# A hybrid attention and recurrence block: three engines in a written order from the output projection to the first FFN tiles, and the first FFN unit's weight sums kept in DRAM

## The chip, the cores and the metric

The kernel runs on one core of a Trainium2 chip. The metric is the device time of one execution in microseconds; the result of a kernel is the median of several executions. A profile is one more execution, taken by the hardware profiler.

## The reference

One layer of a streaming encoder, 512 tokens by 1024 features, in float32:

```python
xn = rmsnorm(h, norm_mix_g)
q, k, v, xr, gr, ga, gb = split(xn @ w_in)
ya = chunked_band_attention(q, k, v, rel_table) @ w_attn_out
yb = (rg_lru(conv(xr)) * gelu(gr)) @ w_rnn_out
h = h + (sigmoid(ga) * ya + sigmoid(gb) * yb) @ w_o
hn = rmsnorm(h, norm_ffn_g)
gate, up = split(hn @ w_ffn_in)           # 2816 columns each
h = h + (silu(gate) * up) @ w_ffn_out
out = rmsnorm(h, final_norm_g)
```

What matters here is the stretch from `@ w_o` to the first columns of `hn @ w_ffn_in`.

## The kernel before

**Precision.** Each float32 factor is split in two: ScalarE writes the rounded part (`hi`, L82), VectorE the rest (`lo`, L83). `mm3` (L74 to L78) then makes three matmuls: hi·hi on L76, hi·lo on L77, lo·hi on L78. So every weight tile that is loaded costs one pass of ScalarE and one of VectorE before TensorE may use it. Weights arrive as `raw` tiles of 128x1024; three such tiles exist, and a fourth load waits until the first is split. All of these loads are issued by SyncE (SP in the profile), one behind the other: a load that waits for its tile holds up those behind it.

**Products in blocks.** The products with `w_o`, and those of the FFN from its second column pair on, use a scheme of seven block products instead of eight (Strassen's, in Winograd's form). The matrices are cut into 2x2 blocks, named 11 to 22 here, and some products use sums of blocks: s1 to s4 of one factor, t1 to t4 of the other. For `w_o` the weights' sums t1 to t4 have been made early in the kernel and stand in DRAM (`sums_o`); b11, b21 and b22 are plain blocks of `w_o`. m is the gated merge that is multiplied with them; its own sums are s1 to s4 (`m_sum`, `m_split`). For the FFN the weights' sums are s1 to s4 (`s_fg`, `s_fu`, two tiles per unit, `s21` and `s34`), made by `weight_sums` from the raw tiles with four VectorE instructions per unit, and t1 to t4 are sums of the activations.

**The stretch in question.** The products with `w_o` are written as `h_multiply` calls, each over two units u: a11·b11, a12·b21, s1·t1, s2·t2, s4·b22, s3·t3, a22·t4. Halves of h (`ht`, four tiles of 128 tokens, h0 to h3) are read out of PSUM by `h_read` (VectorE, L888). When both halves of a token tile are there, `square_h` takes its sum of squares (ScalarE, L896, `hj`), a root follows (L334), a reciprocal (L336), and VectorE scales the tile to `xs_ffn` (L342). `turned` then transposes two feature blocks (`jp`, 0, 2, 4, 6) of two token tiles into one PSUM tile (`pt_ffn`, two of them, TensorE, L349) and evicts it in six pieces: for each of the two blocks a hi by ScalarE (L353) and a lo by VectorE (L354), and a plain float32 copy (`x32`, for the sums t1 to t4) by ScalarE for the first block (L356), by VectorE for the second (L358). The evicted parts are `hn00`, `hn10` (features 0 to 511 and 512 to 1023 of the lower half, tokens of h0 and h1) and `hn01`, `hn11` (the upper half, h2 and h3).

The first FFN columns, `fg0` and `fu0`, are plain products: `project_part` makes four tiles `po_f0` to `po_f3`, each in two halves of 24 matmuls; the lower halves run first, in two parts each, with the upper half's transposes between. The upper halves follow, and then `block_product` (from L269) makes the Strassen tiles in pairs, fg2 and fu2 first. `p` and `q` are its PSUM tiles, `keepa` and `keepb` what ScalarE copies out of `p` and `q` between products, L277.

**What sets the order.** A scheduler orders the instructions of each engine by its own estimate of when they can run. Inside `tc.manual_schedule(engines=...)` the named engines keep the order in which the code is written. In this kernel only TensorE is named; VectorE, ScalarE and SP are placed by the scheduler. In the stretch before the FFN, `barrier[0] = "fg2"` holds loads behind fg2 back.

Late in the FFN, sums of blocks of `w_ffn_out` are made in units (`late`) and written to DRAM; the loop over j advances one of these with `next(steps, None)` twice per pair of tiles.

Of the kernel before, what the change touches and what calls it, by code (L numbers as in the profile page):

```python
# [36 lines left out]
def block_kernel(ctx: ExitStack, tc: tile.TileContext, x, norm_mix_g, w_in, b_merge, rel_table,  # L37
# [118 lines left out]
    begun = {}  # L156
    spare = [None]

    def weight_sums(name, ahead=False):
# [8 lines left out]
        if name not in begun:  # L168
# [3 lines left out]
            s2, s1, s3, s4 = s21[:, 0], s21[:, 1], s34[:, 0], s34[:, 1]  # L172
# [632 lines left out]
    def wo_part(name, src):  # L805
# [38 lines left out]
    for j in range(KT):  # L844
        if j >= 4 and j % 2 == 0:
            blocks_wo(("b11", "b21")[j // 2 - 2])
# [17 lines left out]
    for name in ("t1", "t2", "b22"):  # L864
        blocks_wo(name)
# [10 lines left out]
    def h_multiply(a, b, half, cc, start, tokens=range(2), us=range(2)):  # L876
        for u in us:
            x, w = m_parts[a, u], wo[f"{b}_{u}"]
            for i in tokens:
                tok = slice(i * P, (i + 1) * P)  # L880
                for k in range(2):
                    mm3(bank_of(2 * half + i, cc)[:], x[:, k, 0, tok], x[:, k, 1, tok], w[:, 0, k], w[:, 1, k],
                        start and u == 0 and k == 0, u == 1 and k == 1, parts=True)
# [8 lines left out]
    def square_h(t, cc, last):  # L892
# [4 lines left out]
        if last:  # L897
            q = cp.tile([P, 1], F32, tag="ssq", bufs=4, name=f"hsq{t}")
            dve.tensor_reduce(q[:], q2s[t][:], mybir.AxisListType.X, ALU.add)
            hsq.append(q[:])  # L900

    def finish_h(t, cc, last):
        h_read(t // 2, cc, (t // 2, cc), (t % 2,))
        square_h(t, cc, last)

    with tc.manual_schedule(engines={mybir.EngineType.PE}):
        h_multiply("a11", "b11", 1, 0, True)
        for u in range(2):
# [387 lines left out]
```

## Time and profile before

| | |
|---|---|
| median of 3 runs | 866.77 us (866.61 to 867.26) |
| profiled execution | 866.91 us |
| its span | 865.1 us, TensorE clock 0.997 |
| instructions | 13011 |

The span reaches from the first instruction to the last; the execution's own time is 1.8 us longer. The profile's engines are PE (TensorE), PEld (its weight loads), DVE (VectorE), ACT (ScalarE), POOL (GpSimd) and SP (SyncE). A row of a timeline names start, duration, engine, line, operation, and output and inputs; what stands in brackets is the time that the engine stood idle before, and what ended it. In a group of instructions "x16 | 7.6, 478" means 16 instructions, 7.6 us of busy time together, 478 ns on average.

### The profile page before, as it was taken

Reading aid. Unit: us, or ns where it says so; the run is one execution under the profiler, and the core shown is the slowest. Engines: PE = TensorE matmul, PEld = TensorE weight load, DVE = VectorE, ACT = ScalarE, POOL = GpSimd, SP = SyncE. Lnnn points to the kernel's source line nnn. Section 1 sums busy time; section 2 is a strip of 40 time slices with the busy share of each in tenths; the row PEclk is TensorE's granted clock in tenths of the full one; section 3 lists DMA queues with packets and bytes.
Section 4 is the critical chain, followed back from the end, with each engine's and each line's share of the span. In section 5 each row is a group of like instructions: output and inputs, shape, how many; then the busy total and the mean of one; then the engine's idle time right before and its main releaser. Section 6 shows DMA issues by size and latency. Waiting matters only on the chain.

```text
span 865.1 us, 13011 instructions
## 1 busy us (share of the span) xinstructions
PE 849.9 (98%) x4896; PEld 743.7 (86%) x4896; DVE 632.7 (73%) x973; ACT 505.1 (58%) x869; POOL 97.8 (11%) x135
## 2 busy tenths in 40 slices
PE   8999999999999999999999999999999999999996
PEld 6977887888888888888888888899999999988885
DVE  5789867645666656566558978998988887389973
ACT  7577696741366656576635654564655655374544
POOL 2014202200113313223200000000000001000011
PEclk9999999999999999999999999999999999999998
DMA  8585323439842213232156623857343333295602
GB/s 272 184 304 170 97 73 101 118 94 349 276 134 73 73 48 111 73 110 75 52 167 189 200 75 96 293 169 264 103 124 120 100 98 98 82 318 169 191 20 97
DMA packets 95838, 124.68 MB, mean 144 GB/s; under 512 B 6432, under 2 KB 71568, under 8 KB 95776
## 3 DMA queue, kind: packets, MB, share of 16 engines
q1 hardware_dynamic: 92096, 116.19, 41.4%
q10 hardware_dynamic: 3680, 7.67, 3.3%
q8 instruction: 38, 0.62, 0.3%
q14 instruction: 24, 0.20, 0.1%
HBM read 109.12 MB, written 14.72 MB: 143 GB/s over the span
## 4 chain that ended last, share of the span: by engine, by line
PE 88%; DVE 4%; issue 3%; DMA 2%; ACT 2%; POOL 0%; ACTq 0%; DVEq 0%
PE po_out L76 4%; PE po_out L77 4%; PE po_out L78 4%; PE o L749 2%; PE p_fu L76 2%; PE p_fu L78 2%; PE p_fu L77 2%; PE pT L729 2%; PE p_fg L78 2%; PE p_fg L77 2%; PE p_fg L76 2%; PE po_ga L76 2%; PE po_v L76 2%; PE po_q L76 2%; PE po_ga L78 2%
## 5 line engine op out<-in xcount | busy, mean ns | idle before, releaser
L718 POOL TENSOR_SCALAR p<-p,rl 128x128 f32<-128x128 f32 (+1 forms) x64 | 39.6, 637 | 166.5 <-DVE rl L716 166.4
L715 ACT ACTIVATE p<-p,m 128x128 f32<-128x128 f32 (+1 forms) x64 | 35.8, 562 | 15.3 <-DVE m L714 15.3
L1059 POOL TENSOR_TENSOR act_lo<-act,act_hi 128x1024 fp32r<-128x1024 f32 x1 | 2.4, 2415 | 301.6 <-ACT act_hi L1058 301.6
L83 DVE TENSOR_TENSOR pp<-pT,pp 128x384 fp32r<-128x384 f32 (+1 forms) x48 | 27.8, 596 | 9.8 <-ACT pp L82 9.7
L714 DVE CUSTOM_DVE_ANT_0 p<-s,bias 128x128 f32<-128x128 f32 (+1 forms) x64 | 29.2, 482 | 3.9 <-PE s L711 3.8
L83 DVE TENSOR_TENSOR whl_t<-raw_t,whl_t 128x1024 fp32r<-128x1024 f32 x24 | 29.2, 1219 | 2.8 <-ACT whl_t L82 2.8
L83 DVE TENSOR_TENSOR whl_qk<-raw_qk,whl_qk 128x1024 fp32r<-128x1024 f32 x16 | 21.7, 1359 | 11.2 <-ACT whl_qk L82 11.2
L83 DVE TENSOR_TENSOR whl_fu_s<-s_fu,whl_fu_s 128x1024 fp32r<-128x1024 f32 x20 | 24.3, 1221 | 7.0 <-ACT whl_fu_s L82 6.9
L597 DVE TENSOR_TENSOR spillf<-spillf,spillf 128x1024 f32<-128x1024 f32 x16 | 19.5, 1220 | 12.4 <-DMA spillf<-in_w_ffn_out_dram 9.7
L76 PE MATMUL po_gr<-xnT,whl_gr 128*128 128x512 f32 (+1 forms) x80 | 28.1, 352 | 0.1
L77 PE MATMUL po_xr<-xnT,whl_xr 128*128 128x512 f32 (+1 forms) x80 | 27.8, 353 | 0.0
L77 PE MATMUL po_gr<-xnT,whl_gr 128*128 128x512 f32 (+1 forms) x80 | 27.8, 348 | 0.0
L83 DVE TENSOR_TENSOR whl_fg_s<-s_fg,whl_fg_s 128x1024 fp32r<-128x1024 f32 x20 | 24.3, 1222 | 4.5 <-ACT whl_fg_s L82 4.4
L78 PE MATMUL po_gr<-xnT,whl_gr 128*128 128x512 f32 (+1 forms) x80 | 27.5, 348 | 0.0
L78 PE MATMUL po_xr<-xnT,whl_xr 128*128 128x512 f32 (+1 forms) x80 | 27.3, 346 | 0.0
L76 PE MATMUL po_xr<-xnT,whl_xr 128*128 128x512 f32 (+1 forms) x80 | 26.7, 352 | 0.6 <-ACT xnT L353 0.6
L83 DVE TENSOR_TENSOR whl_b<-raw_b,whl_b 128x1024 fp32r<-128x1024 f32 x18 | 21.9, 1218 | 7.0 <-ACT whl_b L82 6.9
L82 ACT ACTIVATE whl_t<-raw_t 128x1024 fp32r<-128x1024 f32 x24 | 25.1, 1048 | 2.5 <-PE po_out L78 1.6
L82 ACT ACTIVATE whl_b<-raw_b 128x1024 fp32r<-128x1024 f32 x18 | 18.9, 1051 | 12.3 <-DMA raw_b<-in_w_o_dram 12.1
L76 PE MATMUL po_gb<-xnT,whl_gb 128*128 128x512 f32 x64 | 25.1, 392 | 0.5 <-DVE sp_p L452 0.3
L82 ACT ACTIVATE whl_qk<-raw_qk 128x1024 fp32r<-128x1024 f32 x16 | 16.8, 1051 | 15.0 <-PE po_yb L78 8.8
L76 PE MATMUL po_ga<-xnT,whl_ga 128*128 128x512 f32 x64 | 25.3, 395 | 0.0
(386 smaller groups left out, 3251.0 us busy)
## 6 DMA issues: line engine op xcount, KB each, us to landing
raw_fg<-in_w_ffn_in_dram SPq DMA_DIRECT2D x24, 512.0 KB, 3.6
raw_fu<-in_w_ffn_in_dram SPq DMA_DIRECT2D x22, 512.0 KB, 3.5
raw_qk<-in_w_in_dram SPq DMA_DIRECT2D x32, 256.0 KB, 3.3
spillf<-in_w_ffn_out_dram SPq DMA_DIRECT2D x16, 512.0 KB, 7.2
sums<-spillf SPq DMA_DIRECT2D x16, 512.0 KB, 5.2
raw_t<-sums SPq DMA_DIRECT2D x16, 512.0 KB, 4.5
raw_b<-in_w_ffn_out_dram SPq DMA_DIRECT2D x12, 512.0 KB, 4.4
raw_xr<-in_w_in_dram SPq DMA_DIRECT2D x8, 512.0 KB, 4.6
```

The costliest lines, as they stand in the source:

```text
L76: pe.matmul(o, sh, mh, start=start, stop=False, skip_group_check=parts)
L77: pe.matmul(o, sh, ml, start=False, stop=False, skip_group_check=parts)
L78: pe.matmul(o, sl, mh, start=False, stop=stop, skip_group_check=parts)
L82: act.activation(hi, src, AF.Copy)
L83: dve.tensor_sub(lo, src, f(hi))
L597: dve.tensor_sub(out_, a_, b_)
L714: dve.tensor_tensor_reduce(prob[qb][:], scs[qb], bias[:, S - w:S], -1.0, 3e38, ALU.add, ALU.min, nmax[:, qb:qb + 1])
L715: act.activation(prob[qb][:], prob[qb][:], AF.Exp, bias=nmax[:, qb:qb + 1], scale=-1.0, accum_out=lsum[:, qb:qb + 1])
L718: pool.tensor_scalar(prob[qb][:], prob[qb][:], rl[:, qb:qb + 1], 1.0, ALU.mult, ALU.mult)
L729: pe.transpose(pt[:, at * P:(at + 1) * P], prob[qb][:, kb * P:(kb + 1) * P], ident[:])
L749: pe.matmul(po[:, S - n:S], st, pp[i][:, part, lo:lo + n], start=kb == 0 and part == 0, stop=kb == NT - 1 and part == 1)
L1059: (pool if i == 0 else dve).tensor_sub(lo[:], o[:], f(hi[:]))
```

## The change

It has seven parts.

1. The written order covers VectorE and ScalarE too, from a11·b11 to the first activations (`written.close()`).
2. The sums s1 to s4 of fg2 and fu2 are made by `spill_in` during the products with `w_attn_out` (at j = 1 and 2): two loads of 512 KB per unit, four VectorE instructions, four writes of 256 KB to DRAM (`first_sums`). Later `sums_of_first` loads them as two tiles of 512 KB.
3. b22, t1 are loaded and split ahead of the first product, in tiles of their own that earlier stages have left (`v`, `qk`), t2 ahead too; t3 and t4 one product earlier, fu0 between s2·t2 and s4·b22, where it stood at a22·t4.
4. `square_h` and the root and scaling are written one after the other (`summed_h`, `scaled_h`). In the lower half jp 0 and 2 are transposed at the same place as before, then jp 4 and 6 in the middle of a22·t4.
5. The lower FFN halves are no longer cut in two; jp 0 and 2 of the upper half stand behind the second of the four, jp 4 and 6 behind the third. Before, they stood between the parts.
6. fu2's blocks a11 and a12 get tiles as fg2's had.
7. Steps of the late sums of `w_ffn_out` begin at j = 6, where they began at j = 2.

TensorE runs as many matmuls as before. VectorE's instructions go from 969 to 962, ScalarE's from 805 to 806.

```diff
+    def spill_in(name, pl, tag, bufs):
+
+        col = chunks[index[name]][1][0][1]
+        r = [pl.tile([P, 4, CW], F32, tag=tag, bufs=bufs, name=f"spill{name}_{n}") for n in range(2)]
+        for n in range(2):
+            sp.dma_start(out=r[n][:], in_=w_ffn_in[n * S:(n + 1) * S, col:col + CW].rearrange("(k p) e -> p k e", p=P))
+        s2, s3, s4, s1 = (r[n][:, :, i * P:(i + 1) * P] for n in range(2) for i in range(2))
+        dve.tensor_add(s1, s3, s1)
+        dve.tensor_sub(s3, s2, s3)
+        dve.tensor_sub(s2, s1, s2)
+        dve.tensor_sub(s4, s4, s2)
+        for to, of in zip(first_sums[name], ((s2, s1), (s3, s4))):
+            for i in range(2):
+                sp.dma_start(out=to[:, i], in_=of[i])
+
+    def sums_of_first(name):
+        pair = tuple(sums_room.tile([P, 2, 4, P], F32, tag=tag, bufs=1, name=f"{tag}_{name}") for tag in ("s21", "s34"))
+        for t, src in zip(pair, first_sums[name]):
+            sp.dma_start(out=t[:], in_=src[:])
+        return pair
...
     for j in range(KT):
-        if j >= 4 and j % 2 == 0:
-            blocks_wo(("b11", "b21")[j // 2 - 2])
+        if j >= 4:
+            blocks_wo(("b11", "b22", "b21", "t1")[j - 4])
+        if j in (1, 2):
+            spill_in(("fg2", "fu2")[j - 1], aw, "v", 8)
...
-    for name in ("t1", "t2", "b22"):
-        blocks_wo(name)
+    blocks_wo("t2")
...
-    with tc.manual_schedule(engines={mybir.EngineType.PE}):
-        h_multiply("a11", "b11", 1, 0, True)
...
+    written.enter_context(tc.manual_schedule(
+        engines={mybir.EngineType.PE, mybir.EngineType.DVE, mybir.EngineType.Activation}))
+    h_multiply("a11", "b11", 1, 0, True)
+    for u in range(2):
+        m_split("s2", u)
+    h_read(1, 0, (0, 0))
+    blocks_wo("t3")
+    h_multiply("a12", "b21", 0, 0, True)
+    for t in range(2):
+        finish_h(t, 0)
+    for u in range(2):
+        m_split("s4", u)
+    blocks_wo("t4")
+    h_multiply("s1", "t1", 0, 1, True)
+    h_read(0, 1, (1, 1))
+    for u in range(2):
+        m_split("s3", u)
+    weights("fg0", 0)
+    h_multiply("s2", "t2", 1, 0, False)
+    h_read(1, 0, (0, 1))
+    weights("fu0", 0)
+    for t in range(2):
+        h_multiply("s4", "b22", 0, 1, False, (t,))
...
+    finish_h(0, 1)
+    sd = [summed_h(0)]
+    finish_h(1, 1)
+    xs = [scaled_h(0, sd[0])]
+    xs.append(scaled_h(1, summed_h(1)))
+    h_multiply("s3", "t3", 1, 0, False, us=(0,))
+    h_multiply("s3", "t3", 1, 0, False, (0,), us=(1,))
+    h_read(1, 0, (1, 1), (0,))
+    for jp in (0, 2):
+        turned(xs, jp, gf, hn_at, 0, "ffn", f_at)
+    h_multiply("s3", "t3", 1, 0, False, (1,), us=(1,))
+    square_h(2, 1)
+    h_read(1, 0, (1, 1), (1,))
+    square_h(3, 1)
+    split_first("fg2")
+    h_multiply("a22", "t4", 1, 0, False, (0,), us=(0,))
+    turned(xs, 4, gf, hn_at, 0, "ffn", f_at)
+    h_multiply("a22", "t4", 1, 0, False, (0,), us=(1,))
+    finish_h(2, 0)
+    turned(xs, 6, gf, hn_at, 0, "ffn", f_at)
+    xs = [scaled_h(2, summed_h(2))]
+    h_multiply("a22", "t4", 1, 0, False, (1,))
+    finish_h(3, 0)
+    xs.append(scaled_h(3, summed_h(3)))
...
+    for n in range(4):
+        first.append(mm_tile(f"po_f{n}"))
+        part_in(n, 0)
+        if n == 1:
+            act.activation(warm[:], xs[1][:, 0:1], AF.Silu)
+        for jp in ((), (0, 2), (4, 6), ())[n]:
+            turned(xs, jp, gf, hn_at, 1, "ffn", f_at)
...
-        next(steps, None)
+        if j > 4:
+            next(steps, None)
```

**ScalarE, the lower half's evictions and what stands among them.** Rows of before, from the first eviction of the second transposed pair (jp 2) on. `hn00`, `hn10` and `x32` are evictions, `hj` squares, `whl_fu0` a weight split:

```order
L353 ACTIVATE hn00_4584<-pt_ffn0_2_4679,vc_383 128x256
L356 ACTIVATE x32_0_4588<-pt_ffn0_0_4668,vc_383 128x256
L353 ACTIVATE hn00_4584<-pt_ffn0_0_4668,vc_383 128x256
L356 ACTIVATE x32_1_4589<-pt_ffn0_2_4679,vc_383 128x256
L353 ACTIVATE hn00_4584<-pt_ffn0_2_4679,vc_383 128x256
L896 ACTIVATE hj3_1_4702,hsq2_3_4701<-h3_4386 128x512
L353 ACTIVATE hn10_4586<-pt_ffn0_4_4710,vc_383 128x256
L356 ACTIVATE x32_2_4590<-pt_ffn0_4_4710,vc_383 128x256
L353 ACTIVATE hn10_4586<-pt_ffn0_4_4710,vc_383 128x256
L353 ACTIVATE hn10_4586<-pt_ffn0_6_4727,vc_383 128x256
L896 ACTIVATE hj2_0_4739,hsq2_2_4698<-h2_4385 128x512
L82 ACTIVATE whl_fu0_0_4745<-raw_fu0_0_4743 128x1024
```

The same place in the changed kernel (its lines are other ones: L361 is the old L353, L364 the old L356, L929 the old L896, L921 the old L888):

```order
L364 ACTIVATE x32_1_4664<-pt_ffn0_2_4719,vc_383 128x256
L361 ACTIVATE hn00_4659<-pt_ffn0_2_4719,vc_383 128x256
L929 ACTIVATE hj2_1_4737,hsq2_2_4736<-h2_4437 128x512
L929 ACTIVATE hj3_1_4741,hsq2_3_4740<-h3_4438 128x512
L82 ACTIVATE whl_fg2_s2_4747<-s21_fg2_4743 128x2x512
L361 ACTIVATE hn10_4661<-pt_ffn0_4_4756,vc_383 128x256
L364 ACTIVATE x32_2_4665<-pt_ffn0_4_4756,vc_383 128x256
L361 ACTIVATE hn10_4661<-pt_ffn0_4_4756,vc_383 128x256
L929 ACTIVATE hj2_0_4774,hsq2_2_4736<-h2_4437 128x512
L361 ACTIVATE hn10_4661<-pt_ffn0_6_4776,vc_383 128x256
L364 ACTIVATE x32_3_4666<-pt_ffn0_6_4776,vc_383 128x256
L361 ACTIVATE hn10_4661<-pt_ffn0_6_4776,vc_383 128x256
```

A pair's three evictions now stand together. fg2's sums are split between h3's square and jp 4, and h2's second square stands between jp 4 and jp 6, behind which it stood before; the split of fu0 is gone from here.

**VectorE, from the splits of fg0 to the read of h1.** Before (`h` rows are reads out of PSUM, `rs` and `xs` the scaling):

```order
L83 TENSOR_TENSOR whl_fg0_0_4596<-raw_fg0_0_4594,whl_fg0_0_4596 128x1024
L888 SCALAR_TENSOR_TENSOR h0_4383<-po_h2_0_4423,h0_4383 128x512
L888 SCALAR_TENSOR_TENSOR h1_4384<-po_h3_0_4430,h1_4384 128x512
L83 TENSOR_TENSOR whl_fg0_4_4601<-raw_fg0_4_4599,whl_fg0_4_4601 128x1024
L888 SCALAR_TENSOR_TENSOR h0_4383<-po_h0_1_4503,h0_4383 128x512
L899 TENSOR_REDUCE hsq0_4619<-hsq2_0_4482 128x1
L336 RECIPROCAL rs_ffn0_4623<-sd_ffn0_4621 128x1
L342 TENSOR_SCALAR xs_ffn0_4625<-h0_4383,rs_ffn0_4623 128x1024
L888 SCALAR_TENSOR_TENSOR h1_4384<-po_h1_1_4510,h1_4384 128x512
```

Now:

```order
L83 TENSOR_TENSOR whl_fg0_4_4584<-raw_fg0_4_4582,whl_fg0_4_4584 128x1024
L921 SCALAR_TENSOR_TENSOR h0_4435<-po_h2_0_4455,h0_4435 128x512
L921 SCALAR_TENSOR_TENSOR h1_4436<-po_h3_0_4462,h1_4436 128x512
L83 TENSOR_TENSOR whl_fu0_0_4615<-raw_fu0_0_4613,whl_fu0_0_4615 128x1024
L83 TENSOR_TENSOR whl_fu0_4_4620<-raw_fu0_4_4618,whl_fu0_4_4620 128x1024
L921 SCALAR_TENSOR_TENSOR h0_4435<-po_h0_1_4545,h0_4435 128x512
L933 TENSOR_REDUCE hsq0_4670<-hsq2_0_4524 128x1
L921 SCALAR_TENSOR_TENSOR h1_4436<-po_h1_1_4552,h1_4436 128x512
```

The two splits of fu0 now stand ahead of h0's second read, and the read of h1 ahead of h0's scaling.

**SP, the loads behind `w_o`'s last sums.** Before:

```order
L808 DMA raw_t4_0_4535<-sums_o0_3_461 128x1024
L808 DMA raw_t4_1_4540<-sums_o1_3_465 128x1024
L147 DMA raw_fg0_0_4594<-in_w_ffn_in_dram 128x4x256
L147 DMA raw_fg0_4_4599<-in_w_ffn_in_dram 128x4x256
L147 DMA raw_fu0_0_4743<-in_w_ffn_in_dram 128x4x256
L147 DMA raw_fu0_4_4748<-in_w_ffn_in_dram 128x4x256
L147 DMA raw_fg2_0_4865<-in_w_ffn_in_dram 128x4x256
L147 DMA raw_fg2_4_4867<-in_w_ffn_in_dram 128x4x256
```

Now:

```order
L833 DMA raw_t4_1_4540<-sums_o1_3_465 128x1024
L147 DMA raw_fg0_0_4577<-in_w_ffn_in_dram 128x4x256
L162 DMA s21_fg2_4743<-sums_fg2_0_466 128x1024
L162 DMA s34_fg2_4744<-sums_fg2_1_467 128x1024
L147 DMA raw_fg0_4_4582<-in_w_ffn_in_dram 128x4x256
L147 DMA raw_fu0_0_4613<-in_w_ffn_in_dram 128x4x256
L147 DMA raw_fu0_4_4618<-in_w_ffn_in_dram 128x4x256
L147 DMA raw_fg2_0_4999<-in_w_ffn_in_dram 128x4x256
L147 DMA raw_fg2_4_5001<-in_w_ffn_in_dram 128x4x256
```

The tiles s21 and s34 of fg2 are loaded between fg0's two raw tiles, and fu0's loads stand behind.

152 lines of the change are left out of this document (61 added, 91 removed).

## The prediction

> **What bounds the kernel now.** I read the page first: the table of busy time and the chain that ended last.
>
> ```profile
> PE 849.9 (98%) x4896; PEld 743.7 (86%) x4896; DVE 632.7 (73%) x973; ACT 505.1 (58%) x869; POOL 97.8 (11%) x135
> PE 88%; DVE 4%; issue 3%; DMA 2%; ACT 2%; POOL 0%; ACTq 0%; DVEq 0%
> ```
>
> TensorE is busy for 849.9 of 865.1 us and carries the chain. The change leaves its instructions as many as they were, so it moves the end only through the 15.2 us in which TensorE is idle. The next view, windows of 20 us, tells how many of these lie where the change works (columns: TensorE, its weight loads, VectorE, ScalarE, GpSimd, TensorE clock, DMA share, GB/s).
>
> ```profile
> 500.00:520.00 20.00, 19.67 (x109) 16.75 (x108) 14.30 (x30) 11.54 (x29) 0.00 (x0) 1.00 0.23 68
> 520.00:540.00 20.00, 18.11 (x148) 17.32 (x147) 17.15 (x32) 10.25 (x19) 0.00 (x0) 1.00 0.30 90
> 540.00:560.00 20.00, 18.00 (x146) 17.39 (x145) 18.25 (x24) 10.84 (x19) 0.00 (x0) 1.00 0.86 301
> 560.00:580.00 20.00, 20.00 (x169) 20.00 (x168) 19.14 (x27) 11.02 (x21) 0.00 (x0) 1.00 0.46 148
> ```
>
> Idle: 0.33 + 1.89 + 2.00 us between 500 and 560, then none. TensorE's waits from 430 to 566 us name them (us in total, times, longest):
>
> ```profile
> PE pt_ffn L349 <- DVE xs_ffn L342: 1.7, 1, 1.7
> PE q_fg L76 <- ACT keepb_fg L277: 1.0, 1, 1.0
> PE q_fg L76 <- ACT whl_fg_a L82: 0.7, 1, 0.7
> PE pt_ffn L349 <- DVE x L358: 0.3, 1, 0.3
> PE p_fg L76 <- ACT keepa_fg L277: 0.3, 1, 0.3
> ```
>
> 4.0 us. Ends of matmuls are modelled, so a gap reads a little short. Counted from start to start, less the rows' own pitch, the gaps come to about 6.1 us: 1.0 at the transposes of h's upper half and of jp 4 (0.5 each), 2.3 at xs3 and 2.8 in fg2's block products. **Some 6 us is all that this change can win**, so 860.8 us is its floor.
>
> **The work on TensorE around the change.** Its timeline:
>
> ```profile
> 507.25 1.04 PE L349 MATMUL pt_ffn<-ident,xs_ffn 128*128 128x128 f32 x8
> 516.41 0.28 PE L76 MATMUL po_f<-hn,whl_fg 128*128 128x256 f32 x1
> 520.60 0.28 PE L78 MATMUL po_f<-hn,whl_fg 128*128 128x256 f32 x1
> 523.16 0.88 PE L349 MATMUL pt_ffn<-ident,xs_ffn 128*128 128x128 f32 x6 [1.74 <-DVE xs_ffn L342]
> 523.79 0.36 PE L76 MATMUL po_f<-hn,whl_fg 128*128 128x256 f32 x1
> 543.94 0.28 PE L76 MATMUL p_fg<-hn,whl_fg_a 128*128 128x256 f32 x1
> 549.38 0.39 PE L76 MATMUL q_fg<-hn,whl_fg_a 128*128 128x256 f32 x1 [0.72 <-ACT whl_fg_a L82]
> 561.11 0.28 PE L76 MATMUL p_fg<-hn,whl_fg_a 128*128 128x256 f32 x1
> ```
>
> A half f of an FFN tile is 24 matmuls at 0.12 us, 2.88 us. A product follows the one before it without a gap if its hn is evicted. These are the evictions' mean times, from the groups by shape in 500 to 540 us (busy us, mean ns | idle before, releaser):
>
> ```profile
> L354 DVE SCALAR_TENSOR_TENSOR hn<-pt_ffn,vc,hn 128x256 fp32r<-128x256 f32 x16 | 7.6, 478 | 1.8 <-ACT hn L353 1.8
> L353 ACT ACTIVATE hn<-pt_ffn,vc 128x256 fp32r<-128x256 f32 x16 | 7.4, 473 | 4.7 <-PE pt_ffn L349 4.6
> L358 DVE TENSOR_SCALAR x<-pt_ffn,vc 128x256 f32<-128x256 f32 x8 | 3.8, 474 | 0.0
> L356 ACT ACTIVATE x<-pt_ffn,vc 128x256 f32<-128x256 f32 x8 | 3.8, 471 | 2.8 <-DVE hn L354 2.8
> L896 ACT ACTIVATE hj<-h 128x512 f32<-128x512 f32 x6 | 3.8, 632 | 4.1 <-DVE h L888 4.0
> L888 DVE SCALAR_TENSOR_TENSOR h<-po_h,h 128x512 f32<-128x512 f32 x6 | 4.1, 687 | 1.2 <-PE po_h L78 1.2
> L342 DVE TENSOR_SCALAR xs_ffn<-h,rs_ffn 128x1024 f32<-128x1024 f32 x4 | 3.0, 748 | 0.1
> L83 DVE TENSOR_TENSOR whl_fu<-raw_fu,whl_fu 128x1024 fp32r<-128x1024 f32 x2 | 2.4, 1214 | 1.0 <-ACT whl_fu L82 1.0
> L82 ACT ACTIVATE whl_fu<-raw_fu 128x1024 fp32r<-128x1024 f32 x2 | 2.1, 1058 | 0.3 <-PE po_h L78 0.3
> ```
>
> **Part 1: the written order of ScalarE and VectorE.** In the new order a transposed pair's six evictions stand together, and ScalarE's x reads behind VectorE's lo of the same tile. The rows of before show that handover where it already happens:
>
> ```profile
> 512.05 0.47 ACT L353 ACTIVATE hn<-pt_ffn,vc 128x256 fp32r<-128x256 f32 x1 [0.64 <-PE pt_ffn L349]
> 512.55 0.48 DVE L354 SCALAR_TENSOR_TENSOR hn<-pt_ffn,vc,hn 128x256 fp32r<-128x256 f32 x1 [0.54 <-ACT hn L353]
> 513.07 0.47 ACT L356 ACTIVATE x<-pt_ffn,vc 128x256 f32<-128x256 f32 x1 [0.55 <-DVE hn L354]
> ```
>
> Hi at 512.05, lo at 512.55, x at 513.07. A second hi follows the x 0.36 later (the rows overlap by 0.11), its lo 0.50 after that, and VectorE's x 0.39 after the lo. So a pair's chain hangs on both engines in turn, 2.15 us each, 4.90 from the first hi of a pair to the last x of the next. Before put the first hi of jp 2 between those of jp 0, which hid part of this.
>
> In the lower half (tokens 0, 1) I keep the first hi at its time, half a us after the transposes at 507.25. Then jp 0 and 2 end at 507.9 + 4.9 = 512.8, and h3's read (0.69) on VectorE ends at 513.4. ScalarE squares it (0.63), then splits fg2's s2 (1.06) from 514.05 to 515.11, and VectorE's lo (1.22) holds until 516.36. All of this stands ahead of jp 4 on both engines. Jp 4 ends at 518.5, h2's read at 519.1, its square (which stands ahead of jp 6 on ScalarE) at 519.8, and jp 6's last lo at 522.1. TensorE reaches f0 at 516.25, and its blocks 6 and 7 need jp 6: f0 ends at 522.4, not at 516.25 + 2.88 = 519.1. **Stall: +3.3 us**, where before had none. What is taken out ahead of it, fu0's two splits (2.4 us of VectorE), is paid back by s2's (1.2) and by h3's square in the way.
>
> xs3 comes later by the same chain: last x of jp 6 at 522.5; reduce, root, reciprocal and xs2 (0.75) to 523.9; h3's read to 524.5; its square, reduce, root, reciprocal to 526.1; xs3 to 526.8. TensorE is through f1 at 522.4 + 2.88 = 525.3 and waits **1.5 us** (before: 2.3).
>
> In the upper half jp 0's hi starts behind the Silu table load at 527.35, so jp 2's last x ends at 532.25. TensorE is through f2 and jp 4's transposes at 530.8 and waits **1.4 us** for the bank (0.5 in before). Jp 4 and 6 then lie beside f3 and 11.5 us of upper halves; no stall.
>
> **Part 2: the sums made ahead.** They take eight VectorE rows of about 0.69 us out of the stretch from 504 to 545 and put as many beside w_attn_out's products, where VectorE idles about 10 us between 436 and 468 (between splits that wait for ScalarE). They cost nothing there; without that idle time, 5 us of VectorE, which TensorE would see only once its splits are late. What they win is the 2.8 us in fg2's products: q_fg2 and q_fu2 now go first, so the keeps no longer alternate with one bank. What is late next is the first p, which needs a bank that the first Silu frees. Between these stand, on ScalarE, fu2's s2 and s3 splits, and s3 needs s34_fu2, whose load may issue only when fg2's s3 split has freed the single tile (by my schedule at 548.3). For its landing I take these rows:
>
> ```profile
> raw_fg<-in_w_ffn_in_dram SPq DMA_DIRECT2D x10, 512.0 KB, 3.6
> raw_t<-sums_o SPq DMA_DIRECT2D x8, 512.0 KB, 4.7
> raw_b<-in_w_o_dram SPq DMA_DIRECT2D x6, 512.0 KB, 5.7
> ```
>
> At 3.6 to 4.5 the load lands at 551.9 to 552.8. The s3 and a22 splits and a Silu (0.63) follow: the bank is free at 554.2 to 555.0, and TensorE is there at 552.9. **Stall: 1.3 to 2.1**, in place of 2.8.
>
> Sum of these: 0.3 (jp 4's bank in the lower half, 0.5 in before) + 3.3 + 1.5 + 1.4 + 1.7 = 8.2, less 6.1: **+2.1 us**.
>
> **Part 3: raw tiles and the splits moved ahead.** Four more 512 KB loads and eight 256 KB writes stand on SP's queue, whose issues go in order, ahead of ya6's and b22's loads. VectorE in the middle of w_o has no slack:
>
> ```profile
> 485.00:490.00 5.00, 5.00 (x23) 4.13 (x22) 5.00 (x8) 3.81 (x7) 0.00 (x0) 1.00 0.56 167
> 490.00:495.00 5.00, 5.00 (x23) 4.13 (x22) 5.00 (x8) 3.54 (x6) 0.00 (x0) 1.00 0.58 190
> ```
>
> b22's and t1's four splits (1.2 each) leave this stretch; fu0's two enter it, just ahead of h0's second read. These rows mark that place:
>
> ```profile
> 500.64 0.69 DVE L888 SCALAR_TENSOR_TENSOR h<-po_h,h 128x512 f32<-128x512 f32 x1 [0.28 <-PE po_h L78]
> 506.12 0.76 DVE L342 TENSOR_SCALAR xs_ffn<-h,rs_ffn 128x1024 f32<-128x1024 f32 x1
> ```
>
> xs1 ends at 506.88, and the transposes come at 507.25. fu0's second raw tile needs a buffer that fg0's split frees (499.1 + 1.2). If SP has caught up, both come in time: 0. If each load takes the 4.7 to 5.7 of sums and w_o rather than 3.6, h0's read slips from 500.6 to 502.7 at best and 505.2 at worst, xs1 to 509.8, and all that Part 1 counts from 507.25 shifts by up to 2.5. I take **+1.4**, a little over half, since the rows nearest to it are loads of these very queues, at 4.7.
>
> The Trainium skill, page "DMA: Bandwidth & Descriptors", section "Anatomy of one DMA — SWDGE (gpsimd) path", fits 2.0 us plus the bytes at 436 GB/s for loads that GpSimd issues: 3.2 us for 512 KB, an estimate by that page, against 3.6 to 5.7 us in the rows above, which SP issues. By the page's figure this term would be near 0 and the time 868.9; the measured rows decide.
>
> The later spill units (j of 6 and up) fall where TensorE has no gap (20.00 in 560 to 580): 0. In 540 to 560 the DMA queues were 0.86 busy, so there a load that is late or early could cost or save up to 1 us.
>
> **Sum:** 866.91 + 2.1 + 1.4 = 870.4 for a profiled execution (865.1 us span and 1.8 around it). The median of the runs shown is 0.14 below that execution: **870.3 us**.
>
> **Rivals.**
> - *The order does its job* (faster). Fu0's splits (2.4 us of VectorE, 2.1 of ScalarE) and fg2's sums leave the stretch of xs3. If ScalarE and VectorE are ahead of f0, because s2's split finishes before jp 4 is turned, then 3.3 falls to nothing, xs3 is in time (−2.3), jp 4 and 6 too (−0.5), and fg2's 2.8 shrink to 1.7 (−1.1). That gives −3.9: 863.0. For it: VectorE has 2.85 us free in 520 to 540. Against it: s2's split alone takes 2.3 us through both engines and stands in front. It decides from hn10's last lo before 519.
> - *A trade* (no change). Part 3 costs nothing and s34_fu2 lands at once; h3's square is hidden: +2.1 − 1.3 = +0.8, about 867.6.
> - *A longer stall halves the clock* (slower still). Before's longest gap, 1.74 us, left the clock at 1.00 (the windows above). My 3.3 us gap joined with the next one may not: if TensorE ran at half clock for 4 us more, 2 us are lost and with the upper end of Part 3 it is 874. The Trainium skill, page "TensorE: Matmul & The Clock Gate", section "Part 1: The HAM clock gate (the "warmup" mystery)", puts the drop to half clock at one idle window of about 3.4 us; no gap in the trace of before is so long, and the time would be that of this rival.
> - *The order is not what costs.* If the scheduler of before had put these rows in the same places, no term of Part 1 would exist; the order of instructions speaks against it, so it has no chance of its own.
>
> **How the numbers follow.** A measurement of this kernel can tell about 0.2% from no change, 865.0 to 868.5. Forecast, slower, with the long stall: 0.66 (0.05 of it the clock). Trade: 0.15. Faster: 0.19. The upper bounds of the forecast (2.1 + 0.4 + 2.5) give 871.9, with the clock 874.0. The faster case centres on 863.0; half of it lies above, to 864.2. So the range is 864.2 to 874.0; the forecast's own is 868.5 to 872.
>
> **What would show it.** Part 1: TensorE waits of about 3 us in po_f L76 to L78 on hn, released by VectorE's L362, at 518 to 522; xs_ffn3 after 526; a wait at pt_ffn of the upper half on x. If none over 1 us is there, the first rival holds. Part 2: DVE rows on spillfg2 at 436 to 468, and a first p_fg2 that waits for tf0 near 553. Part 3: h0's second read after 502 and a first half transposed after 508. I would be wrong if VectorE's rows ran ahead of TensorE by more than s2's 2.3 us at 514, or if the gain came from upstream of 507.

## The result, and the profile after

The changed kernel takes 876.91 us (median of 4 runs, 875.97 to 878.06) against 866.69 us before: a ratio of 1.0117, 95% interval 1.0100 to 1.0135. It is 10.2 us slower where 3.5 were forecast. The profiled execution took 878.06 us, its span is 876.3 (before: 865.1).

The page's busy times and the windows of 20 us of the changed kernel (columns as in the prediction):

```profile
PE 854.1 (97%) x4896; PEld 746.7 (85%) x4896; DVE 631.8 (72%) x973; ACT 506.5 (58%) x869; POOL 98.0 (11%) x135
```

```profile
500.00:520.00 20.00, 16.99 (x70) 13.26 (x69) 12.58 (x22) 10.37 (x21) 0.00 (x0) 0.83 0.35 113
520.00:540.00 20.00, 16.75 (x122) 15.11 (x121) 11.57 (x27) 9.64 (x23) 0.00 (x0) 1.00 0.09 27
540.00:560.00 20.00, 17.45 (x146) 17.24 (x144) 15.04 (x21) 11.11 (x16) 0.00 (x0) 1.00 0.41 131
560.00:580.00 20.00, 19.41 (x149) 19.42 (x150) 16.74 (x26) 12.13 (x24) 0.00 (x0) 0.91 0.30 87
```

VectorE and ScalarE run as many instructions as in the profile of before, 973 and 869.

TensorE idles 8.8 us between 500 and 560 (before: 4.2). VectorE does less there than before, 39.2 us in place of 49.7, and yet what TensorE needs comes later: xs1 is done at 511.16, before at 506.88. TensorE's granted clock falls to 0.83 and 0.91 in two windows: it is halved for 6.8 us from 509.5 and for 3.4 us from 560.7. The same 4896 matmuls are busy for 4.2 us more, which fits that.

TensorE's waits from 430 to 566, and its timeline at the places where they stand:

```profile
PE pt_ffn L357 <- DVE xs_ffn L942: 4.1, 3, 2.2
PE p_fg L76 <- ACT tf L1042: 3.1, 1, 3.1
PE pt_ffn L357 <- DVE x L366: 1.4, 1, 1.4
PE po_f L76 <- ACT hn L361: 0.4, 1, 0.4
```

```profile
509.76 0.69 PE L357 MATMUL pt_ffn<-ident,xs_ffn 128*128 128x128 f32 x2 [2.24 <-DVE xs_ffn L942]
511.21 1.54 PE L357 MATMUL pt_ffn<-ident,xs_ffn 128*128 128x128 f32 x6 [0.77 <-DVE xs_ffn L942]
512.98 0.63 PE L77 MATMUL po_h<-whl_t,mT 128*128 128x512 f32 x1
513.41 0.63 PE L78 MATMUL po_h<-whl_t,mT 128*128 128x512 f32 x1
```

```profile
560.59 0.50 PE L76 MATMUL p_fg<-hn,whl_fg_a 128*128 128x256 f32 x1 [3.14 <-ACT tf L1042]
560.88 0.42 PE L77 MATMUL p_fg<-hn,whl_fg_a 128*128 128x256 f32 x1
561.10 0.41 PE L78 MATMUL p_fg<-hn,whl_fg_a 128*128 128x256 f32 x1
```

TensorE's start times against those of before: the first FFN matmul is 5.7 us later (522.08, before 516.41), the first block product 7.6, the last run of products with w_ffn_out 9.6, the end of the span 11.2. So about half is lost ahead of the FFN, 1.9 in the lower halves and transposes, 2.0 at the first p product and 1.5 at the tail.

The chain of work that ended last tells more than the waits. Before, it ran over TensorE for 88% of the span. In the changed kernel the profile follows it back to 516. Here is a stretch of it, in order of time (start, us, engine and what):

```profile
518.29 0.96 ACT whl_fg_s L82
519.28 1.23 DVE whl_fg_s L83
520.50 0.41 DVE hn L362
520.93 0.47 ACT x L364
521.41 0.37 ACT hn L361
521.80 0.48 DVE hn L362
522.29 0.39 DVE x L366
...
551.35 1.23 DVE whl_fg_s L83
552.60 5.85 DMA s_fu<-sums_fu
558.50 0.93 issue
559.43 0.61 ACT whl_fu_a L82
560.05 0.49 ACT tf L1042
560.59 0.50 PE p_fg L76
```

From 516 to 560.6 no row of it is TensorE's. It goes back and forth between ScalarE and VectorE, in the written order, down to the load of s34_fu2 (issued at 552.60, landed after 5.85) and the Silu that stands behind that load's split. TensorE's waits are what this chain shows on the outside.

### The profile page after: what moved, and what is told of

The parts are those of the page before. It is cut to its first block, busy times and chain, and to the rows that moved or that the text cites. A ratio compares the mean times of both kernels' runs of the same rounds, so it can differ in the third digit from the quotient of the medians.

```text
span 876.3 us, 13040 instructions
## 1 busy us (share of the span) xinstructions
PE 854.1 (97%) x4896; PEld 746.7 (85%) x4896; DVE 631.8 (72%) x973; ACT 506.5 (58%) x869; POOL 98.0 (11%) x135
## 5 line engine op out<-in xcount | busy, mean ns | idle before, releaser
L83 DVE TENSOR_TENSOR whl_t<-raw_t,whl_t 128x1024 fp32r<-128x1024 f32 x22 | 26.7, 1219 | 2.1 <-ACT whl_t L82 2.0
L82 ACT ACTIVATE whl_fu_s<-s_fu 128x1024 fp32r<-128x1024 f32 x20 | 20.9, 1055 | 10.5 <-DMA s_fu<-sums_fu 5.5
L82 ACT ACTIVATE whl_t<-raw_t 128x1024 fp32r<-128x1024 f32 x22 | 22.9, 1048 | 6.0 <-DMA raw_t<-sums_o 3.4
L76 PE MATMUL po_gb<-xnT,whl_gb 128*128 128x512 f32 x64 | 25.1, 393 | 0.5 <-DVE sp_p L460 0.3
L77 PE MATMUL po_gb<-xnT,whl_gb 128*128 128x512 f32 x64 | 25.2, 393 | 0.0
```

What stands on the lines that cost most here:

```text
L76: pe.matmul(o, sh, mh, start=start, stop=False, skip_group_check=parts)
L77: pe.matmul(o, sh, ml, start=False, stop=False, skip_group_check=parts)
L82: act.activation(hi, src, AF.Copy)
L83: dve.tensor_sub(lo, src, f(hi))
```

## The experiments

**One place at a time.** The first four runs each undo one suspect in the changed kernel.

e1_fu0 moves fu0's splits from ahead of h0's second read to behind xs2:

```diff
     h_read(1, 0, (0, 1))
-    weights("fu0", 0)
...
     xs = [scaled_h(2, summed_h(2))]
+    weights("fu0", 0)
```

> The changed kernel with fu0's two weight splits moved back from ahead of h0's second read to behind xs2. Theory A (these splits, waiting for late raw tiles in a fixed order, hold up h0's read from 500.6 to 506.5 and with it xs0 and xs1, and TensorE's clock halves after the 3 us of waiting): h0's second read near 503.6, xs1 done near 508.2, TensorE waits about 1 us there and the clock stays at 1.00 around 512; the two splits come back 2.4 us before xs3. Time 3 to 4.5 us below the changed kernel, 872.5 to 874. Rival B (the loads are late because of the sums written and read ahead, whatever the order): h0's read stays at 505 or later, time within 1 us of the changed kernel, about 876.5.

Measured: 876.7 us. xs1 was done at 508.17 and not at 511.16, as theory A said, and the first FFN matmul stood at 517.18. Hardly any of it remained in the time: in its trace the two splits stand in front of h3's read instead,

```profile
524.14 0.75 DVE L942 TENSOR_SCALAR xs_ffn<-h,rs_ffn 128x1024 f32<-128x1024 f32 x1
524.89 2.36 DVE L83 TENSOR_TENSOR whl_fu<-raw_fu,whl_fu 128x1024 fp32r<-128x1024 f32 x2
527.17 0.68 DVE L921 SCALAR_TENSOR_TENSOR h<-po_h,h 128x512 f32<-128x512 f32 x1
```

xs3 ended at 530.16 (changed kernel: 531.04), and TensorE waited for hn10 in f0 for 2.0 us. The clock stayed at 1.00 around 512, as theory A said, and was halved for 6.8 us from 522.4 instead. Theory A's place was right, its price was not to be had by itself. Rival B is refuted by h0's earlier read, although its time came true.

e2_evict puts the float32 copies of a pair behind its hi and lo (ScalarE hi, hi, x; VectorE lo, lo, x, with each lo still written right behind its hi):

```diff
             act.activation(hi, pt[:, j], AF.Identity, scale=g[:, jj:jj + 1])
             dve.scalar_tensor_tensor(lo, pt[:, j], g[:, jj:jj + 1], f(hi), ALU.mult, ALU.subtract)
+        for j in range(2):
+            jj = jp + j
             if whole_of and j == 0:
                 act.activation(whole_of(jj, half), pt[:, j], AF.Identity, scale=g[:, jj:jj + 1])
```

> The changed kernel with each transposed pair's float32 copies written behind both hi and lo (hi, hi, x on ScalarE; lo, lo, x on VectorE). Theory (the written order makes a chain of 2.17 us per pair): a pair takes about 1.2 us, the gaps of f0 (1.8 us), of the upper half's first transposes (1.3) and of its jp 6 (1.6) go; time 3.5 to 4.7 us below the changed kernel, 872 to 873.5. Rival (ScalarE and VectorE are late anyway since everything there starts 5 us late): the pair's chain is shorter but the gaps stay above 3 us together, time within 1.2 us of the changed kernel.

Measured: 876.53 us. The theory's edit was a bad one: hi of the second block now waits for lo of the first, so that a pair changes engines five times and not three, and takes 2.46 us and not 2.17. The trace of the changed kernel shows the changes of engine, ScalarE's rows first, then VectorE's:

```profile
511.94 0.47 ACT L361 ACTIVATE hn<-pt_ffn,vc 128x256 fp32r<-128x256 f32 x1 [1.77 <-PE pt_ffn L357]
512.97 0.47 ACT L364 ACTIVATE x<-pt_ffn,vc 128x256 f32<-128x256 f32 x1 [0.55 <-DVE hn L362]
513.34 0.83 ACT L361 ACTIVATE hn<-pt_ffn,vc 128x256 fp32r<-128x256 f32 x2
515.14 0.48 ACT L364 ACTIVATE x<-pt_ffn,vc 128x256 f32<-128x256 f32 x1 [0.97 <-DVE hn L362]
```

```profile
512.45 0.48 DVE L362 SCALAR_TENSOR_TENSOR hn<-pt_ffn,vc,hn 128x256 fp32r<-128x256 f32 x1 [0.69 <-ACT hn L361]
513.84 0.48 DVE L362 SCALAR_TENSOR_TENSOR hn<-pt_ffn,vc,hn 128x256 fp32r<-128x256 f32 x1 [0.91 <-ACT hn L361]
514.24 0.48 DVE L366 TENSOR_SCALAR x<-pt_ffn,vc 128x256 f32<-128x256 f32 x1
```

ScalarE's x (512.97) needs nothing that lo (512.45) makes, and still begins when lo is through: reads of one PSUM tile by ScalarE and VectorE follow one another. The next pair's x (515.14) comes 2.17 us after this one's. The Trainium skill, page "PSUM — Partial Sum Buffer", section "PSUM bank collisions raise a hardware error", says why a program orders them: two engines may not touch the same quadrant of a bank at once, reads included, and the compiler adds a dependency. The trace agrees: from the start of one engine's read to the start of the other's it is 0.50 to 0.52 us (hi 511.94, lo 512.45, x 512.97), where reads of one engine start 0.37 to 0.40 us apart, and for all that time only one of the two engines works on the tile.

e3_silu writes the two Silu ahead of fu2's splits:

```diff
-    weights("fu2", 0)
     act0 = act_tile(0)
-    for c in range(2):
-        tg = swiglu_gate(first[c], c)
+    gates = [swiglu_gate(first[c], c) for c in range(2)]
+    weights("fu2", 0)
+    for c, tg in enumerate(gates):
         dve.tensor_mul(act0[:, c], tg[:], first[2 + c][:])
```

> The changed kernel with the two Silu of the first tiles written ahead of fu2's weight splits. Theory (p's bank is freed by a Silu that stands on ScalarE behind the s3 split, which waits for s34_fu2's load to land at 558.5): the wait of 3.1 us at the first p product goes, and with it the lower clock of 560 to 580 (about 1.6 us); time 4 to 5 us below the changed kernel, 872 to 873. Rival (the late load holds TensorE itself, at the first product with s3): the wait moves to a p product with s3 and stays above 2 us; time within 1 us.

Measured: 876.91 us. The rival was right. The Silu ended at 552, the wait for tf is gone, and two new ones stand in its place, behind the same late load (waits from 430 to 570):

```profile
PE p_fg L76 <- DVE act L1094: 1.1, 1, 1.1
PE q_fg L76 <- ACT whl_fg_a L82: 1.1, 1, 1.1
```

e4_late lets the late sums of w_ffn_out begin at j = 2:

```diff
-        if j > 4:
-            next(steps, None)
+        next(steps, None)
```

> The changed kernel with the late sums of w_ffn_out beginning at j = 2 again. Theory (their later start makes w_ffn_out's first weight splits late at 772, 1.0 us): the two waits of po_out there go, time 1 to 1.5 us below the changed kernel, 875.5 to 876. Rival (a load of these sums collides with fg4's and fu2's loads near 555 if it begins early, which the later start avoids): s34_fu2 lands later than 558.5, time at 877 to 878.

Measured: 876.79 us; of the changed kernel's waits of po_out (0.8 and 0.2 us) the longer one stayed. The later start of these sums is not the cause of the tail's loss, and it did not matter otherwise. That tail stays in every run below, e7_peonly included. In e7_peonly the chain that ended last shows a load of w_ffn_out, the fourth of its plain blocks, that is issued at 749.76 and lands 5.77 us later; before, the fourth was issued at 738.06. Why it is issued later was not tried.

**The chain.** Four edits, each where a wait stood, and each moved the time by less than 0.4 us. So I took the chain itself as theory C, against a common late load (rival D).

e5_evict2 makes a pair change engines once: hi, hi and x on ScalarE, then lo, lo and x on VectorE.

```diff
             act.activation(hi, pt[:, j], AF.Identity, scale=g[:, jj:jj + 1])
+        if whole_of:
+            act.activation(whole_of(jp, half), pt[:, 0], AF.Identity, scale=g[:, jp:jp + 1])
+        for j in range(2):
+            jj = jp + j
+            hi, lo = dst(jj, 0, half), dst(jj, 1, half)
             dve.scalar_tensor_tensor(lo, pt[:, j], g[:, jj:jj + 1], f(hi), ALU.mult, ALU.subtract)
-            if whole_of and j == 0:
-                act.activation(whole_of(jj, half), pt[:, j], AF.Identity, scale=g[:, jj:jj + 1])
-            elif whole_of:
+            if whole_of and j == 1:
                 dve.tensor_scalar(whole_of(jj, half), pt[:, j], g[:, jj:jj + 1], None, ALU.mult)
```

> The changed kernel with each transposed pair evicted as hi, hi, x on ScalarE and then lo, lo, x on VectorE, so that the engines change over once in a pair and not four times. Theory C (from 500 to 560 us one chain through ScalarE and VectorE, in the written order, sets the time, and TensorE's waits only show it; so taking away one wait moves it): two pairs that stand together take 3.5 us in place of 4.9, at three places (jp 0 and 2 of both halves, jp 4 and 6 of the upper half), and all of it comes off the time, 3 to 4 us, to 872.5 to 874. Rival D (what is common to the four runs before is a load that lands late, s34_fu2 and fg4's tiles near 558 to 562, whatever ScalarE and VectorE do): time stays at 876 to 877.

Measured: 869.87 us, ratio 1.0040 (1.0026 to 1.0053): 7.0 us below the changed kernel, more than theory C had said, and rival D is out. Its ScalarE and VectorE rows:

```profile
510.47 0.84 ACT L361 ACTIVATE hn<-pt_ffn,vc 128x256 fp32r<-128x256 f32 x2 [1.52 <-PE pt_ffn L357]
511.19 0.48 ACT L363 ACTIVATE x<-pt_ffn,vc 128x256 f32<-128x256 f32 x1
```

```profile
511.70 0.88 DVE L367 SCALAR_TENSOR_TENSOR hn<-pt_ffn,vc,hn 128x256 fp32r<-128x256 f32 x2 [1.17 <-ACT x L363]
512.49 0.47 DVE L369 TENSOR_SCALAR x<-pt_ffn,vc 128x256 f32<-128x256 f32 x1
512.89 0.86 DVE L367 SCALAR_TENSOR_TENSOR hn<-pt_ffn,vc,hn 128x256 fp32r<-128x256 f32 x2
```

From one pair to the next it is 1.19 us on VectorE in place of 2.17. And in its trace the clock is never halved between 20 and 850 us, which belongs to the 7.0 us too (the table below takes the two apart).

e6_deadline, on top of that, writes h2's last read and square behind jp 6, and fg2's s2 split behind the upper half's jp 4 and 6.

```diff
-    split_first("fg2")
...
-    finish_h(2, 0)
     turned(xs, 6, gf, hn_at, 0, "ffn", f_at)
+    finish_h(2, 0)
...
+        if n == 2:
+            split_first("fg2")
```

> As e5_evict2, and in the lower half h2's last read and square stand behind jp 6, and fg2's s2 split behind the upper half's jp 4 and 6. Theory C: f0 no longer waits for hn10 (2 us gone), xs3 is done 2 to 3 us earlier than in e5_evict2, the s2 split's 2.3 us come back before the bt splits; time 870 to 873. Rival D: 876 to 877.

Measured: 871.69 us, ratio 1.0060 (1.0044 to 1.0076): within what theory C said, and not faster than e5_evict2 (the two intervals overlap) though f0 no longer waited and xs3 was 2.1 us earlier. TensorE came to the first p product at 550.1, 2.6 us earlier, waited there for the Silu, and then ran at a lower clock:

```profile
552.25 0.58 PE L76 MATMUL p_fg<-hn,whl_fg_a 128*128 128x256 f32 x1 [2.13 <-ACT tf L1044]
552.63 0.41 PE L77 MATMUL p_fg<-hn,whl_fg_a 128*128 128x256 f32 x1
552.85 0.41 PE L78 MATMUL p_fg<-hn,whl_fg_a 128*128 128x256 f32 x1
```

Its matmuls follow each other at 0.21 us where 0.12 is usual, for 3.4 us. e5_evict2 came later, did not wait, and was through the same products 1.2 us earlier.

e7_peonly is the changed kernel with TensorE alone in the written order:

```diff
-        engines={mybir.EngineType.PE, mybir.EngineType.DVE, mybir.EngineType.Activation}))
+        engines={mybir.EngineType.PE}))
```

> The changed kernel with the written order for TensorE alone, as before the change; all other parts stay, the sums in DRAM and the loads included. Theory C (the written order of ScalarE and VectorE costs it): the evictions interleave two pairs again, most of the 10 us goes, time 865 to 870. Rival D (the loads and sums cost it): the gaps at xs0/xs1 and at the first p product stay, time 874 to 877.

Measured: 863.13 us, ratio 0.9960 (0.9946 to 0.9973), 13.8 us below the changed kernel and 3.6 below the kernel before: faster than both. All of TensorE's waits from 430 to 566:

```profile
PE pt_ffn L357 <- DVE x L366: 0.3, 1, 0.3
PE pt_ffn L357 <- DVE xs_ffn L942: 0.3, 1, 0.3
```

e8_all is e6_deadline with fu0's splits behind xs3, the Silu ahead of fu2 (as in e3_silu) and the late sums from j = 2 (as in e4_late).

> As e6_deadline, with fu0's splits behind xs3, the two Silu ahead of fu2's splits, and the late sums of w_ffn_out from j = 2. Theory C: with the chain short of TensorE at each place the waits that single edits only moved are gone together: 863 to 868. Rival D: 873 or above.

Measured: 866.73 us, ratio 1.0002 (0.9992 to 1.0012): level with before, and as theory C said.

**Is the chain's length paid, and is the clock?** e11_twice lengthens the chain by a split whose result is there already:

```diff
-        split(o[:, :, 0], o[:, :, 1], begun[name][0][:])
+        for _ in range(2):
+            split(o[:, :, 0], o[:, :, 1], begun[name][0][:])
```

> The changed kernel with the split of fg2's s2 sums done twice, at its place between h3's square and jp 4: one more pass of ScalarE (1.06) and of VectorE (1.22), whose result nobody needs anew. Theory C: the chain is 2.3 us longer and all of it is paid, 879 to 879.6. Rival (ScalarE and VectorE have idle time of 20 of 60 us there, which takes it up): within 0.8 us of the changed kernel, 876 to 877.7.

Measured: 879.4 us (877.6 to 879.5), 2.5 more than the changed kernel, though there VectorE is idle for 20 of the 60 us from 500 to 560 and ScalarE for half of them. That is more than the rival's 0.8, though the intervals (1.0127 to 1.0157, changed kernel 1.0100 to 1.0135) just overlap. The trace is less plain than the median: its chain is 2.1 us longer than the changed kernel's but begins 2.3 us earlier, and what makes this execution longer is that TensorE's clock is halved for 6.8 us behind it and not for 3.4. A cleaner pair is e13_back (below), which has the same order from h0's last read on and the same 6.8 us: there xs1 is done 0.85 us earlier, the chain is 2.3 us shorter, and the profiled execution takes 3.3 us less. Theory C holds.

e9_warm gives TensorE eight matmuls to do while it waits for xs0:

```diff
+        if (name, half, jp) == ("ffn", 0, 0):
+            for _ in range(8):
+                pe.matmul(pt[:].rearrange("p a b -> p (a b)"), ...,
+                          start=True, stop=True, skip_group_check=True)
```

> The changed kernel with eight matmuls of 512 columns more (1.8 us, their result is overwritten), which TensorE makes while it waits for xs0 at 507.5. Both theories: the clock stays at 1.00 around 512 and the products with t3 there take 2.7 us and not 4.8. Theory C (a chain through ScalarE and VectorE sets the time): TensorE only waits longer behind them, for hn10 in f0; time within 0.8 us of the changed kernel, 876 to 877.7. Rival K (the halved clock is paid in full): 2 us below it, near 874.9.

> The kernel of e9_warm once more with more runs, since its four were 872.9 to 880.9. Theory C: median 876 to 877.7, the halved clock around 512 is not paid. Rival K: 874 to 875.5.

Measured: 877.25 us (4 runs, 872.9 to 880.9), then 875.22 (6 runs, 874.6 to 881.2). The ten together have a median of 876.0, between the two theories. In both traces the clock is 1.00 from 500 to 520, the products with t3 take 3.0 us in place of 4.8, and f0 and f1 take longer than in the changed kernel (10.8 and 9.2 us against 7.5): the saved time is not passed on there. The half clock had moved: it stands from 527.9 to 531.3 in the first trace and from 564.7 to 568.1 in the second. What the half clock around 512 costs in the median stays open, between 0 and 2 us.

e12_three is e5_evict2 with fu0's splits behind xs3 and the Silu ahead of fu2.

> As e5_evict2, with fu0's splits behind xs3 and the two Silu ahead of fu2's splits, h2's read and the s2 split at their place in the changed kernel. Theory C (each shortens the chain once the evictions no longer fill it): xs1 near 507, so that the first 2.2 us of waits go, no wait for a Silu: 864.5 to 867. Rival (the two edits only move waits, as they did alone): 869 to 870.5.

Measured: 868.73 us, ratio 1.0025 (1.0014 to 1.0036): 1.1 us below e5_evict2, with intervals that overlap, and neither of the two expected.

e10_pe_evict2 is e7_peonly with the evictions of e5_evict2 in the code.

> As e7_peonly (written order for TensorE alone), with the evictions in the order hi, hi, x, lo, lo, x of e5_evict2 in the code, from which the scheduler starts. Theory C: TensorE has 0.6 us of waits left between 480 and 760 in e7_peonly, so at most that is to be had: 862.3 to 863.3. Rival (the scheduler interleaved two pairs already, and fewer changes of engine only make each lo later): 863.3 to 865.

Measured: 863.21 us, ratio 0.9962 (0.9951 to 0.9974): as e7_peonly. In e7_peonly's trace the scheduler interleaves two pairs, and TensorE's waits there are 0.6 us in all, so there was hardly anything to win.

**Which half of the order.** Three runs begin or end the written order of ScalarE and VectorE at h0's last read (`finish_h(0, 1)`); TensorE's holds throughout. e13_back has it behind that read, e14_front ahead of it, e15_back_evict2 is e13_back with the evictions of e5_evict2.

In the lines below the named engines are all three in e13_back, whose first `manual_schedule` names TensorE alone, and TensorE alone in e14_front.

```diff
+    written.close()
+    written.enter_context(tc.manual_schedule(
+        engines={...}))
     finish_h(0, 1)
```

> The changed kernel with the written order of ScalarE and VectorE beginning only at h0's last read (finish_h(0, 1)); ahead of it TensorE alone is written, as in e7_peonly. Theory C with its seat in the evictions and what follows them: it stays near the changed kernel, 874.5 to 877. Rival U (its seat is upstream, in the splits of t3, t4, fg0 and fu0 between the products with w_o): 865 to 868.

> The other half: ScalarE and VectorE written from the first product with w_o up to the products s4 b22, left to the scheduler behind them. Theory C with its seat in the evictions: most of the 13.8 us between the changed kernel and e7_peonly goes, 863 to 867. Rival U: 873 to 877.

> As e13_back, with the evictions hi, hi, x, lo, lo, x. Theory C: about 7 us below e13_back, as e5_evict2 below the changed kernel, 867 to 870. Rival U: 862 to 865.

Measured: 874.04 us for the back half (ratio 1.0088, 1.0066 to 1.0109), 866.26 for the front half (0.9996, 0.9985 to 1.0007), 869.12 for the back half with the other evictions (1.0018, 1.0006 to 1.0030), 4.9 below the back half where 7 were expected. Against e7_peonly the back half costs 10.9 us and the front half 3.1, together 14.0, and both at once cost 13.8. Rival U is out; about a quarter of the cost is upstream all the same.

The chain's length can be read in each trace, from xs1's end to the issue of s34_fu2. The last three columns are of the profiled execution: its time, from that issue to its end, and how long TensorE's granted clock is halved behind the issue, up to 580.

| run | xs1 done | s34_fu2 issued | between | median us | profiled us | issue to end | half clock |
|---|---|---|---|---|---|---|---|
| changed kernel | 511.2 | 552.6 | 41.4 | 876.9 | 878.1 | 325.5 | 3.4 |
| e3_silu | 511.4 | 552.6 | 41.2 | 876.9 | 877.5 | 324.9 | 3.4 |
| e4_late | 511.4 | 552.6 | 41.2 | 876.8 | 876.6 | 324.1 | 3.4 |
| e13_back | 508.0 | 549.2 | 41.2 | 874.0 | 876.0 | 326.8 | 6.8 |
| e9_warm | 512.4 | 553.8 | 41.4 | 877.3 | 876.5 | 322.7 | 0 |
| e16_warm_again | 514.2 | 555.4 | 41.2 | 875.2 | 881.2 | 325.8 | 3.4 |
| e1_fu0 | 508.2 | 551.7 | 43.6 | 876.7 | 877.4 | 325.7 | 3.4 |
| e2_evict | 509.3 | 552.7 | 43.4 | 876.5 | 877.0 | 324.3 | 3.4 |
| e11_twice | 508.8 | 552.3 | 43.5 | 879.4 | 879.3 | 327.0 | 6.8 |
| e5_evict2 | 509.9 | 545.5 | 35.6 | 869.9 | 868.9 | 323.4 | 0 |
| e15_back_evict2 | 510.2 | 545.8 | 35.6 | 869.1 | 869.1 | 323.4 | 0 |
| e12_three | 508.8 | 546.0 | 37.2 | 868.7 | 868.6 | 322.6 | 0 |
| e6_deadline | 510.0 | 544.6 | 34.6 | 871.7 | 869.8 | 325.2 | 3.4 |
| e8_all | 507.0 | 543.8 | 36.8 | 866.7 | 867.0 | 323.3 | 0 |
| e14_front | 509.4 | 542.4 | 32.9 | 866.3 | 866.2 | 323.9 | 0 |
| e7_peonly | 507.1 | 539.0 | 31.9 | 863.1 | 862.6 | 323.7 | 0 |
| e10_pe_evict2 | 507.4 | 540.2 | 32.8 | 863.2 | 863.2 | 323.1 | 0 |

What is put into this stretch lengthens it by its own time (fu0's splits 2.2, the second s2 split 2.1), whatever TensorE does; the better evictions shorten it by 5.8. The time follows the third column: no later than 546 in every run below 872 us, no earlier than 549 in every run above.

What the third column leaves over is mostly the clock. From the issue to the end it is 322.6 to 323.9 us where the clock is not halved behind the issue, 324.1 to 325.8 with 3.4 us at half clock, and 326.8 to 327.0 with 6.8: half of that time is lost, about 1.7 us for 3.4, and this is read across kernels, not from one edit. Half clock ahead of the issue (6.8 us from 509.5 in the changed kernel, 3.4 in e13_back) does not show in the column between. xs1's end moves too, by 2 us or more between kernels whose order up to there is the same (511.2 in the changed kernel, 508.8 in e11_twice), with the landing of fg0's and fu0's loads.

## Why the prediction was wrong, step by step

- **Right: the side and the mechanism of Part 1.** A pair takes 2.17 us (2.15 forecast). TensorE lost 1.8 us in f0, 1.3 at xs3 and 1.6 at jp 6 where 3.3, 1.5 and 1.4 were forecast.
- **The step that failed is the sum.** It lets the change move the end "only through the 15.2 us in which TensorE is idle", and adds five waits, 0.3 + 3.3 + 1.5 + 1.4 + 1.7 = 8.2, less 6.1, as if each were a price of its own. In the profiled executions TensorE's idle time grew by 7.0 us (15.2 to 22.2), where the sum and Part 3 have 3.5, and its busy time by 4.2, at the lower clock, where they have nothing. And the waits are no prices of their own: they hang on one chain through ScalarE and VectorE. Removing one wait gave 0.0 to 0.2 us (e3, e1), shortening the chain 7.0 (e5, the clock's part included), and taking the written order off ScalarE and VectorE 13.8 (e7).
- **Wrong in size: Part 3.** Forecast +1.4, at most 2.5. xs1 was 4.3 us late and TensorE's products with t3 resumed 4.4 us late. The bounds, h0's read at 502.7 to 505.2, do not come out of the prediction's own rows: there the buffer for fu0's second tile is free at 500.3, and 3.6 us of load, 1.06 of ScalarE's split and 1.2 of VectorE's put the read at 506.2 even with the fastest load. It stood at 506.54. These rows of the changed kernel show it (ScalarE, then VectorE):

```profile
500.09 1.06 ACT L82 ACTIVATE whl_fg<-raw_fg 128x1024 fp32r<-128x1024 f32 x1 [3.20 <-DMA raw_fg<-in_w_ffn_in_dram]
501.51 1.06 ACT L82 ACTIVATE whl_fu<-raw_fu 128x1024 fp32r<-128x1024 f32 x1 [0.36 <-DMA raw_fu<-in_w_ffn_in_dram]
504.30 1.06 ACT L82 ACTIVATE whl_fu<-raw_fu 128x1024 fp32r<-128x1024 f32 x1 [1.73 <-DMA raw_fu<-in_w_ffn_in_dram]
```

```profile
505.40 1.22 DVE L83 TENSOR_TENSOR whl_fu<-raw_fu,whl_fu 128x1024 fp32r<-128x1024 f32 x1 [0.66 <-ACT whl_fu L82]
506.54 0.68 DVE L921 SCALAR_TENSOR_TENSOR h<-po_h,h 128x512 f32<-128x512 f32 x1
```

  fg0's second raw tile is issued at 495.2 and fu0's first at 496.4, when t4's splits free buffers, and fu0's second at 499.9, behind fg0's first split. It lands 4.3 us later, and h0's read stands behind both of its splits. e14_front gives this half 3.1 us.
- **Wrong in size: s34_fu2.** Forecast 1.3 to 2.1 us with a landing in 3.6 to 4.5. It took 5.85, about as long as the longest of the three rows quoted there (5.7), TensorE waited 3.1, and its next 24 matmuls took 1.6 us more at the lower clock.
- **Missed: the tail.** The late units and what follows were put at 0; w_ffn_out's first products lose 1.5 us, in e7_peonly too.
- **The clock.** It had 0.05 of the chances, from a gap over 3.3 us. It fell in a gap of 2.2 us and after one of 3.1, and TensorE is busy 4.2 us longer; of this the table shows only what lies behind the issue, about 1.7 us, as paid. The Trainium skill, page "TensorE: Matmul & The Clock Gate", section "Part 1: The HAM clock gate (the "warmup" mystery)", asks for an idle window of about 3.4 us; here 2.1 us sufficed (e6_deadline).
- **The faster rival** at 863.0 came true in another program: the parts of the change without the order of ScalarE and VectorE give 863.1 (e7_peonly), with fu0 and the sums out of xs3's way.

## What to carry over

Where an order is written for several engines, price it as one chain through all of them, to the load or the bank that its last member frees, and not as a sum of TensorE's waits. Count the changes of engine on each shared PSUM tile: finish one engine's reads before the other's begin, or interleave two tiles. A wait that goes without its time coming back has moved along the chain. Count TensorE's time at half clock behind the chain's end as a price of its own.

## What the runs showed that I had not expected

- TensorE's clock halves after shorter waits than I thought. 256-column matmuls went from 0.12 to 0.21 us for 3.4 us after a wait of 2.13 us (e6_deadline), and 512-column ones from 0.23 to 0.43 after waits of 1.45 and 0.42 us with two transposes between (e14_front); after 1.74 us in the kernel before they did not.
- Eight extra matmuls in such a wait kept the clock at 1.00 there, the half clock came later in both traces, and the time did not clearly follow.
- A load of 512 KB that SP issues took 5.85 us (s34_fu2) beside others. In the other runs the same load took 4.2 (e10_pe_evict2) to 6.4 us (e11_twice).
